# Hybrid decoder layer on one core: the norm's root of the first two chunks of x moved into TensorE's turning product

## The chip, the cores and the metric

The kernel runs on one core of one Trainium2 chip. The metric is the device time of one execution in microseconds, the median of several executions of the same program.

## What is computed

One decoder layer over 512 tokens of width 1024, in float32: a half-step SwiGLU feed-forward block, a token mixer with two kinds of recurrent heads, and a second half-step feed-forward block. Each block stands between two RMS norms. The change touches only the first norm and what follows at once from it.

```python
def rms_norm(x, g):
    y = x * lax.rsqrt(jnp.mean(x * x, axis=-1, keepdims=True) + EPS)
    return y * g

def swiglu_ffn(x, w_in, w_out):
    gate, up = jnp.split(x @ w_in, 2, axis=-1)
    return (jax.nn.silu(gate) * up) @ w_out

x = x + 0.5 * rms_norm(swiglu_ffn(rms_norm(x, norm_pre[0]), ffn1_w_in, ffn1_w_out), norm_post[0])
x = x +       rms_norm(token_mixer(rms_norm(x, norm_pre[1]), ...), norm_post[1])
x = x + 0.5 * rms_norm(swiglu_ffn(rms_norm(x, norm_pre[2]), ffn2_w_in, ffn2_w_out), norm_post[2])
```

## The kernel before

The 512 tokens lie in four chunks of 128, one token per partition, in the tile `xs` (chunk i is `xs[:, i, :]`, with 1024 values per token). Before a product the normed chunk must be turned, so that the 1024 features lie on the partitions. TensorE does this 128x128 block by block against the identity matrix (`turn`, line 353: `transpose`), four blocks, which are one half of a chunk, into one PSUM tile.

Every operand of a product is held as a float32r high part and a float32r low part: ScalarE casts the value (the high part), VectorE subtracts that from the value (the low part), and three products (high by high, high by low, low by high) replace one exact product. A piece of weights goes the same way (`split`: ScalarE's cast in line 283, VectorE's subtraction in line 285). One call of `prod` is 24 such matmuls of 256 columns (line 608).

The feed-forward input product is done in a Strassen-like way on 2x2 halves, so it begins with the products c1, c3, c2, c4 of the list `HEADS`, which need only the first two chunks (`xh[0]`, first half of the features, for c1 and c3; `xh[1]`, second half, for c2 and c4). `start` writes out by hand the order of everything up to there; its calls stand under `tc.manual_schedule()`, so each engine's queue is in the order of the code:

- `gain_pe` loads the norm's gain as one row and spreads it over the partitions with two products against a row of ones; VectorE copies them out (line 177).
- `norm(i)` calls `root` and `scaled`. `root` squares the two halves of a chunk on ScalarE with a sum along the row (line 442), GpSimd turns each sum into a mean (line 443) and takes the power -0.5 (line 447). `scaled` multiplies a half by that root and by the gain on VectorE (line 470).
- `part` is a generator with four steps for one half h of one chunk i: turn, ScalarE's cast (line 373), VectorE's subtraction (line 375), and a plain copy kept for later (line 377).
- `spin` multiplies the identity by itself into a spare PSUM tile; its result is not used (line 183).

The chunks 2 and 3 follow in the middle of the c products (`norm(2)`, `norm(3)`, `to_s`). Weight loads go through SyncE's DMA queue in the order of the code, and a load waits until its buffer's last reader is done.

Of the kernel before, what the change touches and what calls it, by code (L numbers as in the profile page):

```python
# [8 lines left out]
F32 = mybir.dt.float32  # L9
F32R = mybir.dt.float32r  # L10
AF = mybir.ActivationFunctionType
ALU = mybir.AluOpType
PSUM = bass.MemoryType.PSUM

P = 128
T = 512
D = 1024
# [4 lines left out]
EPS = 1e-6  # L22
# [96 lines left out]
class Layer:  # L119
# [43 lines left out]
    def gain_pe(self, tag, row):  # L163

        nc = self.nc
        g = self.cp.tile([P, D], F32, tag=tag, bufs=1, name=self.nm(tag))
        r = self.hf[0:1, 14:16, :].rearrange("p a t -> p (a t)")
        nc.sync.dma_start(r, row)
        one = self.st("one", P)[:1]
        nc.gpsimd.memset(one, 1.0)  # L170
        self.spare = self.ps()
        self.spin(2)
        for h in range(2):
            ps = self.ps()
            v = slice(512 * h, 512 * h + 512)
            nc.tensor.matmul(ps, one, r[:, v], start=True, stop=True)
            nc.vector.tensor_copy(g[:, v], ps)
        return g

    def spin(self, n):  # L180

# [3 lines left out]
    def mm3(self, ps, sh, sl, mh, ml, start, stop, **kw):  # L185
        mm = self.nc.tensor.matmul
        mm(ps, sh, mh, start=start, stop=False, **kw)  # L187
        mm(ps, sh, ml, start=False, stop=False, **kw)  # L188
        mm(ps, sl, mh, start=False, stop=stop, **kw)  # L189

    def xop(self, k, part, t0, t1):
        q = self.xq[2 * (t0 // HALF) + k // KH]
        return q[:, part, k % KH, t0 % HALF : (t1 - 1) % HALF + 1]
# [151 lines left out]
        nc.gpsimd.tensor_tensor(r, m, self.nhalf[:, :n], op=ALU.pow)  # L345
        return r

    def turn(self, src, h):

        pt = self.ps()  # L350
        for c in range(4):
            k = 4 * h + c
            self.nc.tensor.transpose(pt[:, c * P : (c + 1) * P], src[:, k * P : (k + 1) * P], self.ident)  # L353
        return pt.rearrange("p (c t) -> p c t", c=4)

    def two(self, dst, i, src):
# [7 lines left out]
        for h in halves:  # L364
            self.two(self.xq[2 * (i // 2) + h], i, self.turn(src, h))

    def part(self, i, h, src):

        pv = self.turn(src, h)
        v = slice(i * P, (i + 1) * P)  # L370
        dst = self.xh[h][:, :, :, v]
        yield
        self.nc.scalar.copy(dst[:, 0], pv)
        yield
        self.nc.vector.tensor_tensor(dst[:, 1], pv, dst[:, 0].bitcast(F32), op=ALU.subtract)
        yield
        self.nc.scalar.copy(self.xf[h][:, :, v], pv)
        yield
# [39 lines left out]
    def to_s(self, i, src):  # L418

        if i < 2:  # L420
            for h in range(2):
                g = self.part(i, h, src)
                for _ in range(3):
                    next(g)
                self.copies.append(g)
        else:
            self.gs.append(self.sums(i, src))
            next(self.gs[-1])
# [283 lines left out]
        self.hold = ()  # L712
        self.holes()

    def start(self, norm, xn):

        norm(0)
        norm(1)
        q = [[self.part(i, h, xn[i]) for h in range(2)] for i in range(2)]
        step = lambda *gs: [next(g) for g in gs]  # L720
        self.spin(3)
        step(q[0][0], q[0][1], q[0][0])
        self.spin(2)
        split = self.split()
        step(q[1][0], q[1][1])
        next(split)
        step(q[1][0])
        next(split)
        step(q[0][0], q[1][0])
        head = deque(HEADS)  # L730

        def prod():
            p, t = head.popleft()
            self.prod(p, t, False)
            return lambda: self.after(p, t)

        prod()
        self.full_split()
        step(q[0][1], q[1][1], q[0][1], q[1][1])
        prod()  # L740
        self.full_split()
        norm(2)
        c2 = prod()
        self.full_split()
        norm(3)
        step(q[0][0], q[0][1], q[1][0], q[1][1])
        self.full_split()
        self.to_s(2, xn[2])
        c4 = prod()
        c2()  # L750
        self.to_s(3, xn[3])
        p11 = prod()
        self.full_split()
        c4()
        self.lag()
        g2, g3 = self.gs
        prod()
        step(g2)
        p11()
        prod()  # L760
        step(g3)
        self.full_split()
        step(g2)
        e2 = prod()
        step(g3)
        p12 = prod()
        e2()
        self.full_split()
        step(g2)
        step(g3)  # L770
        p21 = prod()
        p12()
        e4 = prod()
        self.full_split()
        p22 = prod()
        p21()
        step(g2)
        step(g3)
        e4()
        self.lag()  # L780
        p22()
        self.holes()
# [1023 lines left out]
def layer(tc, aps):  # L1806
    with ExitStack() as ctx:
        L = Layer(ctx, tc, aps)
        nc = tc.nc
        x, out = aps["x"], aps["out"]  # L1810
        pre, post = aps["norm_pre"][0], aps["norm_post"][0]
        L.weights(
            L.ffn_items("f1", aps["ffn1_w_in"][0], aps["ffn1_w_out"][0]) + L.mix_items()
            + L.ffn_items("f2", aps["ffn2_w_in"][0], aps["ffn2_w_out"][0])
        )
        gp, xn, roots = [None], [None] * NT, {}

        def norm(i, row=None):
            if i == 0 and row is not None:
                gp[0] = L.gain("gpre", pre[row : row + 1, :])  # L1820
            xn[i] = L.pre(i, gp[0], row == 2 and i == NT - 1)

        def root(i):

            if i < 2:
                norm(i, 1)
            else:
                roots[i] = L.root(i)

        def scaled(i, h):  # L1830
            r, xn[i] = roots[i]
            L.scaled(i, gp[0], r, xn[i], h)

        def trans(i):
            L.to_t(i, xn[i])

        def trans_s(i):
            L.to_s(i, xn[i])

        def store(i):  # L1840
            for h in range(2):
                v = slice(512 * h, 512 * h + 512)
                nc.sync.dma_start(out[0, i * P : (i + 1) * P, v], L.xs[:, i, v])

        with ExitStack() as f1:
            L.open_ffn(f1)
            with tc.manual_schedule():
                first = L.start_loads()
                gp[0] = L.gain_pe("gpre", pre[0:1, :])
                for i in range(NT):  # L1850
                    for h in range(2):
                        v = slice(512 * h, 512 * h + 512)
                        (nc.scalar if i < 2 and h else nc.sync).dma_start(L.xs[:, i, v], x[0, i * P : (i + 1) * P, v])
                    if i:
                        L.load(first.popleft())
                    if i == 1:

                        nc.scalar.activation(L.col(), L.nhalf[:, :1], AF.Exp)
                while first:
                    L.load(first.popleft())  # L1860
                L.start(norm, xn)
            L.small_params()
            L.ffn_in()
            L.ffn_out(post[0:1, :], 0.5, root, trans, lambda trans: L.head4(trans, scaled))
        L.mixer()
        with ExitStack() as f2:
            L.open_ffn(f2, True)
            L.mix_out1(lambda i: norm(i, 2), trans_s, L.ffn_head)
            L.ffn_in()
            L.ffn_out(post[2:3, :], 0.5, store, lambda i: None, lambda trans: None)  # L1870
# [30 lines left out]
```

## Time and profile before

| | |
|---|---|
| time, median of 3 runs | 930.09 us (929.65 to 931.55) |
| the profiled execution's own time | 933.69 us |
| its span, first to last instruction | 932.0 us |
| TensorE busy | 921.7 us, 99% of the span |
| VectorE, ScalarE, GpSimd busy | 765.9, 525.2, 186.9 us |
| first product c1 begins | 14.05 us after the span's start |

The profiled execution is one execution with its own time, 3.6 us above the median of the others; sums over its rows are made against that time. In a row of the timeline stand the start, the duration, the engine, the line of the kernel, the operation, output and input, and in brackets how long the engine had been idle before it and what ended that. "PE" is TensorE's matmul, "PEld" its weight load, DVE is VectorE, ACT ScalarE, POOL GpSimd, SP SyncE (SPq is its DMA queue).

### The profile page before, as it was taken

Reading aid. Unit: us, or ns where it says so; the run is one execution under the profiler, and the core shown is the slowest. Engines: PE = TensorE matmul, PEld = TensorE weight load, DVE = VectorE, ACT = ScalarE, POOL = GpSimd, SP = SyncE. Lnnn points to the kernel's source line nnn. Section 1 sums busy time; section 2 is a strip of 40 time slices with the busy share of each in tenths; the row PEclk is TensorE's granted clock in tenths of the full one; section 3 lists DMA queues with packets and bytes.
Section 4 is the critical chain, followed back from the end, with each engine's and each line's share of the span. In section 5 each row is a group of like instructions: output and inputs, shape, how many; then the busy total and the mean of one; then the engine's idle time right before and its main releaser. Section 6 shows DMA issues by size and latency. Waiting matters only on the chain.

```text
span 932.0 us, 18308 instructions
## 1 busy us (share of the span) xinstructions
PE 921.7 (99%) x7423; PEld 887.4 (95%) x7423; DVE 765.9 (82%) x992; ACT 525.2 (56%) x757; POOL 186.9 (20%) x256
## 2 busy tenths in 40 slices
PE   8999999999999999999999999999999999999997
PEld 7999999999999999998887888899999999999997
DVE  5899978889888776698847564799898989998886
ACT  6645455557565466956633444495454545756661
POOL 3531112121111045452321210304000000011002
PEclk9999999999999999999999999999999999999999
DMA  9245679776797925798742124452453435279542
GB/s 310 76 138 157 181 182 214 195 157 142 209 273 238 262 65 150 151 184 208 152 98 69 46 72 132 137 162 66 135 159 123 136 111 174 84 221 261 165 153 91
DMA packets 118766, 145.42 MB, mean 156 GB/s; under 512 B 7413, under 2 KB 91417, under 8 KB 118682
## 3 DMA queue, kind: packets, MB, share of 16 engines
q1 hardware_dynamic: 102714, 129.05, 44.2%
q0 software_dynamic: 15680, 14.69, 11.6%
q8 instruction: 58, 0.95, 0.4%
q10 hardware_dynamic: 288, 0.52, 0.2%
q14 instruction: 26, 0.21, 0.1%
HBM read 142.14 MB, written 31.46 MB: 186 GB/s over the span
## 4 chain that ended last, share of the span: by engine, by line
PE 62%; ACT 1%; DVE 0%; issue 0%; POOL 0%; DVEq 0%; POOLq 0%; ACTq 0%
PE ps L608 22%; PE ps L955 8%; PE ps L538 6%; PE ps L187 5%; PE ps L189 5%; PE ps L188 5%; PE ps L947 4%; PE ps L1373 2%; PE ps L353 1%; PE ps L548 1%; PE ps L1466 0%; PE ps L1671 0%; PE ps L1644 0%; PE ps L1419 0%; PE ps L1668 0%; PE ps L1431 0%
## 5 line engine op out<-in xcount | busy, mean ns | idle before, releaser
L283 ACT CAST w<-raw 128x1024 fp32r<-128x1024 f32 x246 | 251.3, 1028 | 199.0 <-PE ps L608 93.6
L285 DVE TENSOR_TENSOR w<-raw,w 128x1024 fp32r<-128x1024 f32 x246 | 298.9, 1219 | 30.9 <-ACT w L283 29.5
L608 PE MATMUL ps<-xq,w 128*128 128x256 f32 x2016 | 237.1, 277 | 0.0
L608 PEld LDWEIGHTS ps<-xq,w 128*128 128x128 f32 x2016 | 232.9, 188 | 0.0
L608 PE MATMUL ps<-sq,w 128*128 128x256 f32 x1512 | 178.0, 276 | 0.3
L608 PEld LDWEIGHTS ps<-sq,w 128*128 128x128 f32 x1512 | 174.2, 188 | 1.0 <-ACT ps L659 0.9
L299 DVE TENSOR_TENSOR raw<-raw,raw 128x1024 f32<-128x1024 f32 x72 | 89.8, 1251 | 7.8 <-DMA raw<-in_ffn_w_in_dram 6.1
L955 PE MATMUL ps<-w,hs 128*128 128x256 f32 x672 | 81.0, 276 | 0.0
L947 PE MATMUL ps<-w,hs 128*128 128x256 f32 x672 | 79.2, 276 | 0.0
L955 PEld LDWEIGHTS ps<-w,hs 128*128 128x128 f32 x672 | 78.4, 188 | 0.0
L187 PE MATMUL ps<-w,xq 128*128 128x512 f32 x192 | 77.9, 407 | 0.1
L947 PEld LDWEIGHTS ps<-w,hs 128*128 128x128 f32 x672 | 77.5, 188 | 0.0
L189 PE MATMUL ps<-w,xq 128*128 128x512 f32 x192 | 74.8, 391 | 0.0
L188 PE MATMUL ps<-w,xq 128*128 128x512 f32 x192 | 74.8, 390 | 0.0
L538 PE MATMUL ps<-xq,w 128*128 128x256 f32 x480 | 57.5, 282 | 0.0
L538 PEld LDWEIGHTS ps<-xq,w 128*128 128x128 f32 x480 | 56.6, 189 | 0.5 <-issue 0.5
L887 POOL DMA_DIRECT2D f2sums<-in_ffn_w_out_dram x15 | 20.0, 1482 | 176.9 <-DMA f2sums<-in_ffn_w_out_dram 176.9
L827 ACT CAST hs<-hf 128x1024 fp32r<-128x1024 f32 x32 | 33.7, 1053 | 28.8 <-PE ps L955 21.1
L828 DVE TENSOR_TENSOR hs<-hf,hs 128x1024 fp32r<-128x1024 f32 x32 | 39.1, 1221 | 8.7 <-ACT hs L827 8.2
L887 POOL DMA_DIRECT2D f1sums<-f1sums x26 | 23.2, 892 | 105.9 <-DMA f1sums<-in_ffn_w_out_dram 53.0
L187 PEld LDWEIGHTS ps<-w,xq 128*128 128x128 f32 x192 | 36.1, 188 | 8.5 <-issue 1.0
L189 PEld LDWEIGHTS ps<-w,xq 128*128 128x128 f32 x192 | 36.1, 188 | 8.1 <-DVE xq L360 0.3
(262 smaller groups left out, 1223.3 us busy)
## 6 DMA issues: line engine op xcount, KB each, us to landing
raw<-in_ffn_w_in_dram SPq DMA_DIRECT2D x98, 512.0 KB, 5.3
raw<-in_ffn_w_out_dram SPq DMA_DIRECT2D x44, 512.0 KB, 4.5
raw<-in_w_mix_in_dram SPq DMA_DIRECT2D x28, 512.0 KB, 3.6
raw<-f2sums SPq DMA_DIRECT2D x15, 512.0 KB, 5.6
raw<-f1sums SPq DMA_DIRECT2D x13, 512.0 KB, 7.6
raw<-in_w_mix_out_dram SPq DMA_DIRECT2D x8, 512.0 KB, 3.7
f2sums<-in_ffn_w_out_dram SPq DMA_DIRECT2D x30, 128.0 KB, 5.9
f2sums<-in_ffn_w_out_dram SPq DMA_DIRECT2D x15, 256.0 KB, 5.7
```

What stands on the lines that cost most here:

```text
L187: mm(ps, sh, mh, start=start, stop=False, **kw)
L188: mm(ps, sh, ml, start=False, stop=False, **kw)
L189: mm(ps, sl, mh, start=False, stop=stop, **kw)
L283: nc.scalar.copy(hi, raw)
L285: self.low = nc.vector.tensor_tensor(lo, raw, hi.bitcast(F32), op=ALU.subtract)
L299: added = (nc.vector if late else nc.gpsimd).tensor_tensor(o, o, c, op=ALU.add)
L538: mm(ps[:, u0:u1], w[:, a, k, :], self.xop(k, b, u0, u1), start=k + n + m == 0, stop=k == ND - 1 and n == 2, skip_group_check=True,)
L608: self.nc.tensor.matmul(ps[:, c], wb[b][:, k, v], left[d][:, k, :], start=first and a + n + k == 0, stop=n == 2 and k == KH - 1, skip_grou ...
L828: self.nc.vector.tensor_tensor(lo, src, hi.bitcast(F32), op=ALU.subtract)
L887: nc.gpsimd.dma_start(to[:, a:b], v, accum_op=ALU.add)
L947: mm(out, a[kk][:, i * P : (i + 1) * P], w[:, b, kk, QUARTER * v : QUARTER * (v + 1)], start=begin and c == kk == n == 0, stop=kk == 1 and ...
L955: mm(ps[:, QUARTER * c : QUARTER * (c + 1)], A[a][:, c], B[b], start=begin and c == n == 0, stop=n == 2, skip_group_check=True,)
```

## The change

For chunks 0 and 1 only:

- ScalarE squares a chunk whole (`root_whole`: two instructions of 1024 columns instead of four of 512), and GpSimd makes one mean and one power of each.
- VectorE multiplies x by the gain alone (`scale`), half by half, without waiting for the root. The copy of the gain's second half comes after the first halves of both chunks (`rest`).
- VectorE multiplies the identity by the root, one root per partition (`diagonal`), and `turn` multiplies each block by this diagonal with an ordinary float32 `matmul` in place of `transpose`. The turned block comes out scaled.
- Only the first halves are turned before c1. The second halves of both chunks are turned between c1 and c3; VectorE's `scale(1, 1)` stands after the subtractions of the first halves.
- ScalarE's cast of the first piece of weights stands before the casts of the first halves, no longer between them.

```diff
     def gain_pe(self, tag, row):
...
-            nc.vector.tensor_copy(g[:, v], ps)
-        return g
+            copies.append(lambda v=v, ps=ps: nc.vector.tensor_copy(g[:, v], ps))
+        copies[0]()
+        return g, copies[1]
...
-    def turn(self, src, h):
+    def turn(self, src, h, diag=None):
...
-            self.nc.tensor.transpose(pt[:, c * P : (c + 1) * P], src[:, k * P : (k + 1) * P], self.ident)
+            out, block = pt[:, c * P : (c + 1) * P], src[:, k * P : (k + 1) * P]
+            if diag is None:
+                self.nc.tensor.transpose(out, block, self.ident)
+            else:
+                self.nc.tensor.matmul(out, block, diag, start=True, stop=True)
...
-    def start(self, norm, xn):
-
-        norm(0)
-        norm(1)
-        q = [[self.part(i, h, xn[i]) for h in range(2)] for i in range(2)]
+    def root_whole(self, i):
+
+        nc = self.nc
+        out = self.hf[:, 2 * i : 2 * i + 2, :].rearrange("p a t -> p (a t)")
+        ss, m, r = self.col(), self.col(), self.col()
+        nc.scalar.activation(out, self.xs[:, i, :], AF.Square, accum_out=ss)
+        nc.gpsimd.tensor_scalar(m, ss, 1.0 / D, EPS, op0=ALU.mult, op1=ALU.add)
+        nc.gpsimd.tensor_tensor(r, m, self.nhalf[:, :1], op=ALU.pow)
+        return r
+
+    def start(self, norm, xn, g, rest):
...
+        def scale(i, h):
+            v = slice(512 * h, 512 * h + 512)
+            nc.vector.tensor_tensor(src[i][:, v], self.xs[:, i, v], g[:, v], op=ALU.mult)
+
+        def diagonal(i):
+            nc.vector.tensor_scalar(diag[i], self.ident, roots[i], None, op0=ALU.mult)
+
+        scale(0, 0)
+        scale(1, 0)
+        rest()
+        roots = [self.root_whole(i) for i in range(2)]
+        diag = [self.st("diag", P) for _ in range(2)]
+        diagonal(0)
+        scale(0, 1)
+        diagonal(1)
+        q = [[self.part(i, h, src[i], diag[i]) for h in range(2)] for i in range(2)]
         step = lambda *gs: [next(g) for g in gs]
+        split = self.split()
+        next(split)
         self.spin(3)
-        step(q[0][0], q[0][1], q[0][0])
+        step(q[0][0], q[0][0])
         self.spin(2)
-        split = self.split()
-        step(q[1][0], q[1][1])
-        next(split)
-        step(q[1][0])
+        step(q[1][0], q[1][0])
         next(split)
         step(q[0][0], q[1][0])
+        scale(1, 1)
...
         prod()
         self.full_split()
-        step(q[0][1], q[1][1], q[0][1], q[1][1])
+        step(q[0][1], q[1][1], q[0][1], q[1][1], q[0][1], q[1][1])
```

On TensorE, from the last spins before the first turn to c2. Before (`xn_170` is the normed chunk 0, `hf_113` holds chunk 1, `ps_220` is c1 and then c2, `ps_253` is c3):

```order
4 L183 MATMUL ps_131<-ident 128x128 x3
5 L353 MATMUL ps_190<-ident,xn_170 128x128 x4
6 L353 MATMUL ps_195<-ident,xn_170 128x128 x4
7 L183 MATMUL ps_131<-ident 128x128 x2
8 L353 MATMUL ps_203<-ident,hf_113 128x128 x4
9 L353 MATMUL ps_208<-ident,hf_113 128x128 x4
10 L608 MATMUL ps_220<-xq_78,sq_116 128x256 x24
11 L608 MATMUL ps_253<-xq_78,sq_114 128x256 x24
12 L608 MATMUL ps_220<-xq_75,w 128x256 x24
```

The same place after the change (`xn_157` and `hf_113` hold the two chunks times the gain, `diag_173` and `diag_174` the diagonals, `ps_202` is c1 and then c2, `ps_245` is c3):

```order
4 L185 MATMUL ps_131<-ident 128x128 x3
5 L359 MATMUL ps_182<-diag_173,xn_157 128x128 x4
6 L185 MATMUL ps_131<-ident 128x128 x2
7 L359 MATMUL ps_190<-diag_174,hf_113 128x128 x4
8 L614 MATMUL ps_202<-xq_78,sq_116 128x256 x24
9 L359 MATMUL ps_231<-diag_173,xn_157 128x128 x4
10 L359 MATMUL ps_236<-diag_174,hf_113 128x128 x4
11 L614 MATMUL ps_245<-xq_78,sq_114 128x256 x24
12 L614 MATMUL ps_202<-xq_75,w 128x256 x24
```

The turns of the two second halves moved from ahead of c1 to between c1 and c3, and all four turns are now products with a diagonal.

On VectorE, from the first copy of the gain to the subtraction for the second piece of weights. Before (`sq_116` and `sq_114` are the pieces of weights of c1 and c3, `xq_78` is the turned first half):

```order
1 L177 COPY gpre_127<-ps_134 128x512
2 L177 COPY gpre_127<-ps_137 128x512
3 L470 SCALAR_TENSOR_TENSOR xn_170<-xs,col_168,gpre_127 128x512 x2
4 L470 SCALAR_TENSOR_TENSOR hf_113<-xs,col_183,gpre_127 128x512 x2
5 L285 TENSOR_TENSOR sq_116<-raw_119,sq_116 128x1024
6 L375 TENSOR_TENSOR xq_78<-ps_190,xq_78 128x4x128
7 L375 TENSOR_TENSOR xq_78<-ps_203,xq_78 128x4x128
8 L285 TENSOR_TENSOR sq_114<-raw_121,sq_114 128x1024
```

After the change:

```order
1 L178 COPY gpre_127<-ps_134 128x512
2 L739 TENSOR_TENSOR xn_157<-xs,gpre_127 128x512
3 L739 TENSOR_TENSOR hf_113<-xs,gpre_127 128x512
4 L178 COPY gpre_127<-ps_136 128x512
5 L742 TENSOR_SCALAR diag_173<-ident,col_163 128x128
6 L739 TENSOR_TENSOR xn_157<-xs,gpre_127 128x512
7 L742 TENSOR_SCALAR diag_174<-ident,col_169 128x128
8 L287 TENSOR_TENSOR sq_116<-raw_119,sq_116 128x1024
9 L381 TENSOR_TENSOR xq_78<-ps_182,xq_78 128x4x128
10 L381 TENSOR_TENSOR xq_78<-ps_190,xq_78 128x4x128
11 L739 TENSOR_TENSOR hf_113<-xs,gpre_127 128x512
12 L287 TENSOR_TENSOR sq_114<-raw_121,sq_114 128x1024
```

The four multiplications by root and gain became four by the gain alone, two of them ahead of the root; two small products of the identity with a root came in, and the last half of chunk 1 moved behind the subtractions of the first halves.

On SyncE's queue three loads changed places: the two small loads `gb` and the gain of the norm behind the block (`gpost`, 512 KB) now stand before two pieces of weights (`raw_37`, `raw_316`) that they followed.

More of the change, by code (lines that the diff above doesn't have):

```diff
@@ L172, in gain_pe @@
         self.spin(2)
+        copies = []
         for h in range(2):
@@ L365, in to_t, with part @@
             self.two(self.xq[2 * (i // 2) + h], i, self.turn(src, h))
-    def part(self, i, h, src):
-        pv = self.turn(src, h)
+    def part(self, i, h, src, diag):
+        pv = self.turn(src, h, diag)
         v = slice(i * P, (i + 1) * P)
@@ L421, in to_s @@
             for h in range(2):
-                g = self.part(i, h, src)
+                g = self.part(i, h, src, None)
                 for _ in range(3):
@@ L713, in ffn_head @@
         self.holes()
-    def start(self, norm, xn):
-        norm(0)
-        norm(1)
-        q = [[self.part(i, h, xn[i]) for h in range(2)] for i in range(2)]
+    def root_whole(self, i):
[7 more added lines that the diff above has]
+    def start(self, norm, xn, g, rest):
+        nc = self.nc
+        src = [self.sp.tile([P, D], F32, tag="xn", bufs=1, name=self.nm("xn"))]
+        src.append(self.hf[:, 16:18, :].rearrange("p a t -> p (a t)"))
+        def scale(i, h):
[12 more added lines that the diff above has]
+        q = [[self.part(i, h, src[i], diag[i]) for h in range(2)] for i in range(2)]
         step = lambda *gs: [next(g) for g in gs]
+        split = self.split()
+        next(split)
         self.spin(3)
-        step(q[0][0], q[0][1], q[0][0])
+        step(q[0][0], q[0][0])
         self.spin(2)
-        split = self.split()
-        step(q[1][0], q[1][1])
-        next(split)
-        step(q[1][0])
+        step(q[1][0], q[1][0])
         next(split)
         step(q[0][0], q[1][0])
+        scale(1, 1)
         head = deque(HEADS)
@@ L1848, in layer @@
                 first = L.start_loads()
-                gp[0] = L.gain_pe("gpre", pre[0:1, :])
+                gp[0], rest = L.gain_pe("gpre", pre[0:1, :])
                 for i in range(NT):
@@ L1860, in layer @@
                     L.load(first.popleft())
-                L.start(norm, xn)
+                L.start(norm, xn, gp[0], rest)
             L.small_params()
```

## The prediction, written before the changed kernel ran

> **What bounds the kernel now.** I read the page's sums first, then the windows, then what TensorE waits for.
>
> ```profile
> span 932.0 us, 18308 instructions
> PE 921.7 (99%) x7423; PEld 887.4 (95%) x7423; DVE 765.9 (82%) x992; ACT 525.2 (56%) x757; POOL 186.9 (20%) x256
> ...
> 0.00:14.05 14.05, 10.54 (x35) 7.24 (x35) 5.64 (x8) 6.55 (x14) 3.99 (x17) 1.00 0.84 284
> 14.05:400.00 385.95, 385.75 (x3369) 384.70 (x3370) 326.47 (x392) 236.56 (x328) 104.55 (x129) 1.00 0.67 178
> ...
> 500.00:925.00 425.00, 424.56 (x3347) 406.73 (x3345) 353.06 (x469) 230.95 (x346) 44.46 (x72) 1.00 0.43 133
> ...
> PE ps L353 <- DVE xn L470: 1.7, 1, 1.7
> PE ps L183 <- POOL ident masks.py:199: 1.6, 1, 1.6
> PE ps L608 <- ACT xq L373: 0.2, 1, 0.2
> ```
>
> From 14.05 us on, where the first product c1 begins, TensorE (first busy column) works 385.75 of 385.95 us, later 424.56 of 425. All its named waits lie before 14.05. So the time is the start of c1, plus TensorE's work behind it, plus a tail that the change does not touch. A microsecond less before c1 is a microsecond won, and a microsecond of TensorE work put behind c1 is one lost, unless something waits there.
>
> The timeline of the opening shows how c1's start comes about.
>
> ```profile
> 6.39 0.63 ACT L442 ACTIVATE junk<-xs 128x512 f32<-128x512 f32 x1 [3.20 <-DMA xs<-in_x_dram]
> 6.42 1.65 PE L183 MATMUL ps<-ident 128*128 128x128 f32 x6
> 6.53 0.69 DVE L177 COPY gpre<-ps 128x512 f32<-128x512 f32 x1 [1.02 <-PE ps L176]
> 7.14 0.63 ACT L442 ACTIVATE junk<-xs 128x512 f32<-128x512 f32 x1
> 7.68 0.19 ACT L442 ACTIVATION_READ_ACCUMULATOR junk<-xs 128x1 f32 x1
> 8.39 0.56 POOL L447 TENSOR_TENSOR col<-col,nhalf 128x1 f32<-128x1 f32 x1
> 8.98 1.41 DVE L470 SCALAR_TENSOR_TENSOR xn<-xs,col,gpre 128x512 f32<-128x512 f32 x2 [1.76 <-POOL col L447]
> 9.03 0.75 POOL L443 TENSOR_SCALAR col<-col 128x1 f32<-128x1 f32 x1
> 9.79 1.97 PE L353 MATMUL ps<-ident,xn 128*128 128x128 f32 x8 [1.72 <-DVE xn L470]
> 11.42 1.05 ACT L283 CAST sq<-raw 128x1024 fp32r<-128x1024 f32 x1
> 11.55 1.06 PE L183 MATMUL ps<-ident 128*128 128x128 f32 x4
> 12.40 1.41 PE L353 MATMUL ps<-ident,hf 128*128 128x128 f32 x8
> 13.41 0.59 ACT L373 CAST xq<-ps 128x512 fp32r<-128x512 f32 x1 [0.94 <-PE ps L353]
> 14.05 5.83 PE L608 MATMUL ps<-xq,sq 128*128 128x256 f32 x48 [0.24 <-ACT xq L373]
> ```
>
> x arrives at 6.39; squares, mean and power give VectorE the root at 8.98; TensorE turns from 9.79. From there TensorE itself is the chain: 8 transposes and 4 spin instructions take 9.79 to 12.40 (the four spins 12.40 - 11.55 = 0.85, 0.213 us each); chunk 1's first half follows, ScalarE casts it at 13.41, and c1 starts 0.64 us later. c1 and c3 (x48) run without a gap between them.
>
> **The change part by part.** First, what a turn costs now.
>
> ```profile
> L183 PE MATMUL ps<-ident 128*128 128x128 f32 x14 | 3.9, 443 | 1.6 <-POOL ident masks.py:199 1.6
> L176 PE MATMUL ps<-hf,one 1*128 1x512 f32 x4 | 3.8, 1096 | 0.0
> 441.14 1.95 PE L1419 MATMUL ps<-q,kk 128*128 128x128 f32 x16
> 442.85 0.48 PE L187 MATMUL ps<-w,xq 128*128 128x512 f32 x1
> 22.44 1.03 PE L353 MATMUL ps<-ident,xn 128*128 128x128 f32 x8
> ```
>
> The code spins 7 times, and the group has 14 instructions; the gain is spread by 2 products, with 4. An ordinary float32 product is thus two passes, where eight transposes are eight instructions. Later in the kernel a pass is faster: 16 passes of 128x128 take 442.85 - 441.14 = 1.71 us, 0.107 each, half of the 0.213 in the opening. The eight transposes at 22.44 (1.03 us) against those at 9.79 (1.97) say the same. Each turned half therefore grows from 4 passes to 8.
>
> *Start of c1.* Squaring whole: a half takes 0.63; a cast of 1024 columns takes 1.05 where one of 512 takes 0.59, so the whole square takes about 0.63 + 0.46 = 1.09 and its sum is read out by 6.39 + 1.09 + 0.10 = 7.58, against 7.87 for the second half before. From 7.87 to VectorE's 8.98 it took 1.11 us; the same gives 8.69. VectorE has by then done two `scale` halves and the gain's second copy (three times 0.69 from 6.39: 8.46). The diagonal is a quarter of such a copy's columns; no row shows one, so it lies between 0 and 0.69, and I take 0.25 by the column count. TensorE starts at 9.0, 0.8 us earlier. But before, c1 needed 4 + 4 + 4 + 4 = 16 slow passes (two turned halves, spins, one half); now it needs 8 + 4 + 8 = 20. Before: 9.79 + 16 x 0.213 = 13.20, cast at 13.41. Now: 9.0 + 20 x 0.213 = 13.26, cast at 13.47, c1 at 14.11. **Term: +0.06.** The 0.8 us gained ahead of the turns go into four more passes.
>
> Chunk 1's root does not decide: its mean may wait beside VectorE's `scale(0, 1)`, as the 0.75 us of POOL's 9.03 row beside the 8.98 row shows, so its diagonal comes at about 10.5; TensorE gets to it only at 9.0 + 12 x 0.213 = 11.6.
>
> When TensorE speeds up matters too. The eight transposes at 12.40 took 1.41, between 1.97 and 1.03: the pace changed at about 13.1, 3.3 us after TensorE's steady work began at 9.79 (the granted clock reads 1.00 throughout and does not show it). If the change comes 3.3 us after steady work begins, it comes at 12.3 now, and the 0.96 us of passes behind it halve: c1 0.5 earlier, and the sum below is +1.5. If it comes at the same moment as before, the sum stands at +2.0. I take the second, as spins ran in both just ahead, and keep the first as the lower end. [...]
>
> *The second halves.* Before, TensorE turned chunk 0's second half in passes already counted, and chunk 1's while it would have waited for the cast. Now both stand between c1 and c3, where it never waited: 2 x 4 blocks x 2 passes = 16 passes of 128x128, the same as the 441.14 row. **Term: +1.71.** Slow passes would make it 3.4, but by 17 us the pace is the fast one.
>
> *What is late behind.* ScalarE and VectorE do the rest of the opening in a fixed order, and these rows are its slack.
>
> ```profile
> 14.84 1.07 ACT L373 CAST xq<-ps 128x512 fp32r<-128x512 f32 x2
> 15.80 1.07 ACT L283 CAST w<-raw 128x1024 fp32r<-128x1024 f32 x1
> 19.62 1.42 DVE L470 SCALAR_TENSOR_TENSOR xn<-xs,col,gpre 128x512 f32<-128x512 f32 x2 [1.09 <-POOL col L447]
> 20.95 1.22 DVE L285 TENSOR_TENSOR sq<-raw,sq 128x1024 fp32r<-128x1024 f32 x1
> 22.19 0.37 SPq L244 DMA_DIRECT2D raw<-in_ffn_w_in_dram  x1
> 22.88 1.41 DVE L470 SCALAR_TENSOR_TENSOR hf<-xs,col,gpre 128x512 f32<-128x512 f32 x2 [0.72 <-POOL col L447]
> 26.14 1.04 PE L353 MATMUL ps<-ident,hf 128*128 128x128 f32 x8
> 31.56 4.89 POOL L299 TENSOR_TENSOR raw<-raw,raw 128x1024 f32<-128x1024 f32 x2 [1.16 <-DVE w L285]
> ```
>
> The casts of the second halves (14.84) now wait for their turns: c1 ends at about 16.8, the turns at 18.6, the second cast at 19.3, where the next piece's cast started at 15.80 before. What queues behind them on ScalarE, the squares of chunks 2 and 3 above all, is 3.5 us later. Chunk 2, scaled by 21.04 before, is scaled by about 24.5; TensorE wants to turn it at 22.44 + 1.77 = 24.2. A slack of 1.4 us becomes a wait of 0.3, give or take as much: **term +0.2** (0 to 0.6). Chunk 3, scaled by 24.3, comes at 27.8 against a turn at 26.14 + 2.0 = 28.1: just in time.
>
> *The rest costs nothing.* ScalarE's cast of the first weights now stands ahead of the first halves' casts and waits for a transfer:
>
> ```profile
> 2.08 0.43 SPq L244 DMA_DIRECT2D raw<-in_ffn_w_in_dram  x1
> DMA to landing us min/median/max: 6.8/7.7/8.8
> ```
>
> It lands between 8.9 and 11.3, is cast by 12.4 at the latest, and the cast that c1 needs comes at 13.47. VectorE's `scale(1, 1)` (0.7) has until c1 ends. SyncE's load that was issued at 22.19, when VectorE's row of 20.95 had freed its buffer, goes out at about 25.7 behind the gain's 512 KB and lands by 34.9; POOL's second addition in the 31.56 row is its first reader, at 34.0 before and about 37 now.
>
> *Sum.* 0.06 + 1.71 + 0.2 = +2.0 us. The profiled execution would go from 933.69 (span 932.0 and 1.7 around it) to 935.7. It lies 3.6 above the median of the runs shown; I carry the difference over: 930.09 + 2.0 = **932.1**. A measurement of this kernel can tell about 0.2%, 1.86 us, from no change, so this stands just beyond it.
>
> **The rivals.**
>
> *The fast pace comes a whole stretch earlier (not slower), 0.20.* TensorE now pauses only from 8.07 to 9.0 between spins and turns, not to 9.79, and everything it does is a full product. If that suffices to bring the pace up by 9.75, 16.5 of the 20 passes take 0.107: 9.75 + 1.77 = 11.5, c1 at 11.5 + 0.85 = 12.4, and -1.65 + 1.71 + 0.2 = +0.3: 930.4. It decides if the pace changes before about 11. Against it: 8 transposes and 4 spin instructions were enough to bring it up before. [...]
>
> *x arrives earlier in the other executions (slower still), 0.17.* They are 3.6 us faster than the profiled one, whose ScalarE waited for x until 6.39. With x there by 4.4, TensorE turns once the spins end at 8.07, in both kernels; then c1 starts at 8.07 + 3.41 + 0.85 = 12.3 before and 8.07 + 4.26 + 0.85 = 13.2 now. +0.85 + 1.71 + 0.2 = +2.8: 932.9.
>
> *More waits behind, 0.08.* ScalarE is 3.5 us late and TensorE 2.0; wherever less than 1.5 us of slack is left, TensorE waits. Chunk 3 has 0.3. Up to 1 us more: 933.1.
>
> *The product with the diagonal is one pass, like a transpose, 0.05.* Then c1 needs 12 passes: 9.0 + 2.56 + 0.85 = 12.4, and the second halves cost 0.86: -1.65 + 0.86 + 0.2 = -0.6, 929.5. The 14 instructions of 7 spins speak against it.
>
> **How the numbers follow.** The forecast has 0.50, with its own range +1.3 to +2.6 (the earlier pace, the wait of 0 to 0.6). Range for 8 in 10: from the early pace with a little less, 930.0, to the largest of the slower cases, 933.3. Slower by over 0.2%: about 0.62 of the forecast's 0.50, and the 0.17 and 0.08, 0.56. Faster by over 0.2% takes an early pace and a cheap turn together, or something not seen here: 0.07. Within: 0.37.
>
> **What would show it.** Right: TensorE's turns start near 9.0 with x8 in place of x4 instructions a half, c1 within 0.3 of 14.1, a row of 16 product instructions taking 1.7 between c1 and c3, chunk 2's turn waiting for VectorE. Wrong: c1 before 13, the fast pace ahead of 11, the second halves' turns under 1 us, or idle time on TensorE in front of c3.

## The result and the profile after

| | |
|---|---|
| kernel before, median of 6 runs | 930.57 us (929.65 to 931.55) |
| changed kernel, median of 6 runs | 935.72 us (933.0 to 937.5) |
| ratio | 1.0053, interval 1.0035 to 1.0072 |
| profiled execution of the changed kernel | 935.71 us, span 934.0 us |

The change costs 5.15 us where 2.0 were predicted, and the median lies 2.4 us above the range. First the page's sums for the changed kernel (busy time of each engine).

```profile
span 934.0 us, 18329 instructions
PE 924.0 (99%) x7439; PEld 889.3 (95%) x7439; DVE 767.4 (82%) x994; ACT 524.5 (56%) x753; POOL 185.5 (20%) x254
```

Its windows with c1's start as the cut (length, then busy time of PE, PEld, DVE, ACT, POOL, granted clock, DMA share, GB/s):

```profile
13.52:400.00 386.48, 386.30 (x3370) 384.92 (x3371) 326.64 (x391) 234.52 (x326) 103.94 (x130) 1.00 0.68 178
```

What TensorE waits for (total, times, longest), but for the identity at the start:

```profile
PE ps L359 <- DVE diag L742: 0.8, 1, 0.8
PE ps L614 <- ACT xq L379: 0.7, 1, 0.7
```

TensorE is still full from c1 on (386.30 of 386.48), so the bound was read rightly. It pauses twice ahead of c1: 0.8 us for the diagonal, 0.7 for the cast. The timeline of the opening says why.

```profile
4.83 1.06 ACT L726 ACTIVATE hf<-xs 128x1024 f32<-128x1024 f32 x1 [1.64 <-DMA xs<-in_x_dram]
6.48 0.56 POOL L728 TENSOR_TENSOR col<-col,nhalf 128x1 f32<-128x1 f32 x1
7.36 0.69 DVE L739 TENSOR_TENSOR hf<-xs,gpre 128x512 f32<-128x512 f32 x1 [1.12 <-DMA xs<-in_x_dram]
7.97 0.68 DVE L178 COPY gpre<-ps 128x512 f32<-128x512 f32 x1
8.57 0.28 DVE L742 TENSOR_SCALAR diag<-ident,col 128x128 f32<-128x128 f32 x1
8.91 2.07 PE L359 MATMUL ps<-diag,xn 128*128 128x128 f32 x8 [0.83 <-DVE diag L742]
13.52 3.02 PE L614 MATMUL ps<-xq,sq 128*128 128x256 f32 x24 [0.68 <-ACT xq L379]
16.38 1.05 PE L359 MATMUL ps<-diag,xn 128*128 128x128 f32 x8
18.08 3.05 PE L614 MATMUL ps<-xq,sq 128*128 128x256 f32 x24
```

Here x of chunk 0 is squared from 4.83, not from 6.39 as in the execution that the prediction was worked from, and the root of chunk 0 is out by 7.04. But VectorE stands at chunk 1's product (7.36) and waits 1.12 us for chunk 1's x; the gain's copy and the diagonal come behind it in its queue. So TensorE turns from 8.91, when it could have turned at 8.0, the end of its spins (before_again, below). The second halves of both chunks cost 18.08 - 16.38 = 1.70.

### The profile page after: what moved, and what is told of

Its sections match the earlier page's. It is cut to its first block, busy times and chain, and to the rows that moved or that the text cites. A ratio compares the mean times of both kernels' runs of the same rounds, so it can differ in the third digit from the quotient of the medians.

```text
span 934.0 us, 18329 instructions
## 1 busy us (share of the span) xinstructions
PE 924.0 (99%) x7439; PEld 889.3 (95%) x7439; DVE 767.4 (82%) x994; ACT 524.5 (56%) x753; POOL 185.5 (20%) x254
## 4 chain that ended last, share of the span: by engine, by line
PE 56%; DVE 3%; issue 1%; POOL 1%; ACT 1%; DMA 1%; DVEq 0%; POOLq 0%; ACTq 0%
PE ps L614 16%; PE ps L988 8%; PE ps L544 6%; PE ps L189 5%; PE ps L191 5%; PE ps L190 5%; PE ps L980 4%; PE ps L1406 2%; DVE w L287 1%; PE ps L554 1%; POOL raw L301 1%; PE ps L357 1%; DVE raw L301 1%; DMA raw<-in_ffn_w_in_dram 1%; PE ps L1499 0%
```

## The experiments

These explanations stand against each other in the expectations. A: the profiled execution of the kernel before had a late x and others don't, and the changed kernel is held by chunk 1's x on VectorE. B: executions differ only in the moment at which TensorE's passes become fast; P, in later expectations: pauses on TensorE move that moment. C: waits behind c1. The kernel before was measured again beside every set; its medians there were 930.81, 931.27, 931.27 and 932.03 us.

**Both kernels again.** *before_again* is the kernel before, *after_again*, *after_timed* and *after_x1_late* are the changed kernel, all four unaltered (the last label means a base for the kernels with a later x below).

> The kernel before, unchanged, for a second profile of it and as a measure of how far two sets of executions of one program lie apart (ratio 1.000, within 0.1%). Theory A (x comes earlier in most executions than in the profile shown, and the kernel before uses that while the changed one does not): this profile has the first square before 5.5 us and c1 before 12.8, and its own time is nearer 930.5 than 933.7. Theory B (only the moment of the fast pace differs between executions): the first square again near 6.4, c1 near 14, the own time moved by the pace alone. Theory C (waits behind c1 make the difference): c1 as in the first profile, own time near 933.7.

> The changed kernel, unchanged, for a second profile. In the first one TensorE's first turn began at 8.91, after VectorE had waited until 7.36 for chunk 1's first half, and the pace rose at about 12. Theory A: the first turn again waits for chunk 1's half, whatever chunk 0 does, so it begins 8.5 to 9.2; c1 13 to 14.2; own time 933 to 937.5. Theory B: the own time goes with the pace alone, about 0.5 us for each us that the pace rises later. Theory C: named waits of TensorE behind c1.

> The changed kernel once more, unaltered, timed in rounds beside the kernel before: how wide its executions scatter, and its own x4.x profile for a third time. [...]

> The changed kernel unaltered (the name notwithstanding), as the base for the next one on the same chip. Theory A: its time follows the landing of chunk 1's first half: 933.4 to 934.5 with the first turn at 7.9 to 8.1 if that lands by 6.3, 935 to 936.5 with the first turn at 8.7 or later if it lands by 7.2.

before_again took 931.04 us (ratio 1.0002, 0.9993 to 1.001); its profiled execution has a span of 929.3 against the first one's 932.0. Its timeline:

```profile
4.62 0.63 ACT L442 ACTIVATE junk<-xs 128x512 f32<-128x512 f32 x1 [1.43 <-DMA xs<-in_x_dram]
8.02 1.97 PE L353 MATMUL ps<-ident,xn 128*128 128x128 f32 x8
10.63 1.70 PE L353 MATMUL ps<-ident,hf 128*128 128x128 f32 x8
12.36 5.84 PE L608 MATMUL ps<-xq,sq 128*128 128x256 f32 x48
```

x is there at 4.62, TensorE turns at once when its spins end at 8.02, and c1 starts at 12.36, not 14.05. The execution behind the prediction was one with a late x. The changed kernel took 936.1 (one execution), 933.87 (ratio 1.003, 1.0018 to 1.0041) and 933.41 (1.0023, 1.0011 to 1.0034). Chunk 1's product, the first turn and c1 in the timelines, of after_again, of after_timed and of after_x1_late:

```profile
7.24 0.69 DVE L739 TENSOR_TENSOR hf<-xs,gpre 128x512 f32<-128x512 f32 x1 [1.00 <-DMA xs<-in_x_dram]
8.78 2.08 PE L359 MATMUL ps<-diag,xn 128*128 128x128 f32 x8 [0.71 <-DVE diag L742]
13.75 3.11 PE L614 MATMUL ps<-xq,sq 128*128 128x256 f32 x24 [0.68 <-ACT xq L379]
```

```profile
6.19 0.69 DVE L739 TENSOR_TENSOR hf<-xs,gpre 128x512 f32<-128x512 f32 x1
7.89 1.92 PE L359 MATMUL ps<-diag,xn 128*128 128x128 f32 x8
11.88 3.05 PE L614 MATMUL ps<-xq,sq 128*128 128x256 f32 x24 [0.68 <-ACT xq L379]
```

```profile
6.24 0.68 DVE L739 TENSOR_TENSOR hf<-xs,gpre 128x512 f32<-128x512 f32 x1
7.95 1.91 PE L359 MATMUL ps<-diag,xn 128*128 128x128 f32 x8
12.44 3.10 PE L614 MATMUL ps<-xq,sq 128*128 128x256 f32 x24 [0.68 <-ACT xq L379]
```

One kernel, two kinds of opening: with chunk 1's x at 7.24 the first turn waits 0.71 for the diagonal and c1 is 1.39 behind before_again's; with x at 6.19 or 6.24 it waits for nothing, and c1 is 0.48 ahead or 0.08 behind. That chunk 1's x can hold the first turn is shown by that; the 0.56 between the two early ones is mostly the pace: TensorE's passes became fast at about 9.8 in after_timed (four spins in 0.71 us from 9.60) and at about 10.9 in after_x1_late (four in 1.06 from 9.66, then the eight passes of chunk 1 in 1.26 from 10.51; at the fast pace eight take 1.06).

Two expectations missed. after_timed was to have a median of 935.0 to 936.5, and had 933.87 with executions 1.8 us apart. And after_x1_late's profiled execution, with its early first turn, was to take 933.4 to 934.5, and took 935.47, 2.1 over the median of its own set. So the landing of chunk 1's x alone doesn't tell how long an execution takes.

**One line moved on VectorE.** *x1_behind* is the changed kernel with chunk 1's product behind chunk 0's diagonal:

```diff
         scale(0, 0)
-        scale(1, 0)
         rest()
...
         diagonal(0)
+        scale(1, 0)
```

> The changed kernel with the product of chunk 1's first half and the gain moved behind chunk 0's diagonal on VectorE, so that chunk 1's x no longer stands in front of chunk 0's turn. Theory A (that order costs the time before c1 and, through the pause on TensorE, the early pace): 1 to 2 us faster than the changed kernel, ratio to before 1.003 to 1.004; first turn by 8.1 when the spins end. Theory B or C: as the changed kernel, ratio 1.005.

It took 932.98 us (1.0028, 1.0017 to 1.0039), beside 936.1 of after_again on the same chip. But 936.1 is one execution, and the unaltered kernel stands as near to the kernel before in the other two sets (1.003 and 1.0023). So no gain in time is shown here. TensorE didn't wait for a diagonal (timeline), but chunk 1's first half may have been early, too:

```profile
7.97 1.81 PE L359 MATMUL ps<-diag,xn 128*128 128x128 f32 x8
```

**Chunk 1's x made later.** In *before_x1_late* (kernel before), *after_x1_later* (changed) and *x1_behind_later* (x1_behind) its first half is issued behind the first weight load, not ahead of it:

```diff
                 for i in range(NT):
+                    if i == 1:
+                        L.load(first.popleft())
                     for h in range(2):
...
-                    if i:
+                    if i > 1:
                         L.load(first.popleft())
```

> The kernel before with one thing moved: chunk 1's first half of x is issued behind the first weight load instead of ahead of it, so that it lands about 1.3 us later (7.4 to 8.5 where the traces so far show 5.8 to 7.3). Chunk 1's turn came 3.9 us after its squares began in the trace of before_again (6.74 to 10.63), 0.85 of it filled by spins. Theory A (chunk 1's x decides only where it stands ahead of chunk 0's diagonal): c1 0 to 0.9 later than 12.36, median 0 to 1.2 over the kernel before.

> The changed kernel with chunk 1's first half of x issued behind the first weight load, about 1.3 us later. Theory A: VectorE stands at the product of chunk 1's first half until it lands and does the gain's copy (0.69) and the diagonal (0.28) only then, so that the first turn starts 1.5 us after the landing, at 9.0 to 10.0, with a pause of 1 to 2 us on TensorE ahead of it, and c1 6.5 us after the landing, at 14 to 15; median 3.5 to 6.5 over the kernel before, 2 to 3.5 more than the same shift costs the kernel before. Theory C (fixed waits behind c1): no more than the kernel before loses by the shift.

> x1_behind (the product of chunk 1's first half behind chunk 0's diagonal on VectorE) with the same later landing. Theory A: the first turn stays at 8.0, the filling products lie ahead of the landing's effect, c1 0.3 to 0.9 later than its 11.80, median 1.8 to 3.2 over the kernel before and at least 1.5 under after_x1_later. Theory C: the same as after_x1_later.

They took 932.87 (1.0016, 1.0006 to 1.0026), 935.83 (1.0045, 1.0028 to 1.0061) and 933.51 us (1.003, 1.0019 to 1.0041). The shift costs the kernel before 1.6 (0 to 1.2 were expected), the changed one 2.4 (from 933.41). That is 0.8 more, where I had expected 2 to 3.5 more: a miss. With the product behind the diagonal the time is 2.3 lower on the same chip (933.51 against 935.83; at least 1.5 was expected). The timelines, of after_x1_later and then of x1_behind_later:

```profile
9.34 0.69 DVE L739 TENSOR_TENSOR hf<-xs,gpre 128x512 f32<-128x512 f32 x1 [2.99 <-DMA xs<-in_x_dram]
10.55 0.27 DVE L742 TENSOR_SCALAR diag<-ident,col 128x128 f32<-128x128 f32 x1
10.88 2.07 PE L359 MATMUL ps<-diag,xn 128*128 128x128 f32 x8 [2.70 <-DVE diag L742]
16.18 3.10 PE L614 MATMUL ps<-xq,sq 128*128 128x256 f32 x24 [0.68 <-ACT xq L379]
```

```profile
7.86 1.77 PE L359 MATMUL ps<-diag,xn 128*128 128x128 f32 x8
7.96 0.69 DVE L739 TENSOR_TENSOR hf<-xs,gpre 128x512 f32<-128x512 f32 x1 [0.55 <-DMA xs<-in_x_dram]
12.30 3.04 PE L614 MATMUL ps<-xq,sq 128*128 128x256 f32 x24 [0.68 <-ACT xq L379]
```

The diagonal comes 1.21 us behind the product's start in both executions with a late x (7.36 to 8.57, 9.34 to 10.55), and TensorE waits for it; in x1_behind_later it turns at 7.86, before chunk 1's x is there at 7.96. So the hold on VectorE is shown, and that the order is worth time when x is late. My 1.5 us from landing to first turn held (9.34 to 10.88). The x came later than I thought here, and the same edit left it at 7.96 in the other execution, so the two c1 compare the order and the landing together.

**The second halves alone.** *late_halves* and *late_again* are the kernel before (transposes, split squares) with only the second halves turned late; *late_filled* is the same with three pauses of TensorE filled by unused products (the notes behind # say where; they don't stand in the code).

```diff
         self.spin(3)            # late_filled: spin(5)
-        step(q[0][0], q[0][1], q[0][0])
+        step(q[0][0], q[0][0])
         self.spin(2)            # late_filled: spin(3)
...
-        step(q[1][0], q[1][1])
+        step(q[1][0])
...
         step(q[0][0], q[1][0])  # late_filled: spin(3) behind it
...
-        step(q[0][1], q[1][1], q[0][1], q[1][1])
+        step(q[0][1], q[1][1], q[0][1], q[1][1], q[0][1], q[1][1])
```

> The kernel before with one part of the change alone: the second halves of chunks 0 and 1 are turned (by transposes of the normed chunk, as before) between c1 and c3. It moves 8 one-pass blocks behind c1, 0.86 us by the fast pace, and takes 4 passes from in front of c1 (0.4 to 0.85) if the roots are there in time. Theory A or B: +0.3 to +0.9 us, ratio 1.000 to 1.001. Theory C (the casts that wait behind the late turns make TensorE wait): +1.5 to +2.5 us, ratio 1.002 to 1.003.

> late_halves once more, as the base for late_filled on the same chip. Theory P: in the executions in which TensorE's pauses (0.4, 0.3 and 0.7 us ahead of c1) move the change of pace behind c1, c1's 24 passes take 5.5 us instead of 2.9: 933 to 936 with a scatter of 5 us or more. Theory C: 933 to 936 with a scatter like the kernel before's (4 us or less).

> late_halves with the three pauses filled by passes that nothing uses (two filling products more ahead of the first turn, one more ahead of chunk 1's, three ahead of c1; 12 instructions). Theory P: the fast pace comes by 13 us in every execution, c1's 24 passes take 2.9 to 3.1 us, c1 at 12.3 to 13.3, median 931.8 to 933.3 and the slowest executions under 935, though TensorE runs 12 passes more. Theory C: no gain, 0 to 1 us slower than late_again.

late_halves took 934.36 us (1.004, 1.0023 to 1.0057; 931.2 to 939.12), late_again 934.18 (1.0025, 1.0011 to 1.0039; 931.46 to 937.2), late_filled 932.34 (1.0006, 0.9996 to 1.0016; 931.16 to 934.39). I had expected 0.3 to 0.9 over the kernel before for the first and missed. Twelve instructions more on the full engine made it 1.8 us faster. What TensorE waits for in late_halves:

```profile
PE ps L608 <- ACT xq L373: 0.7, 1, 0.7
PE ps L353 <- DVE xn L470: 0.4, 1, 0.4
PE ps L353 <- DVE hf L470: 0.3, 1, 0.3
```

The timelines, of late_halves, of late_again and of late_filled:

```profile
12.48 5.49 PE L608 MATMUL ps<-xq,sq 128*128 128x256 f32 x24 [0.67 <-ACT xq L373]
17.77 0.72 PE L353 MATMUL ps<-ident,xn 128*128 128x128 f32 x4
```

```profile
12.14 3.05 PE L608 MATMUL ps<-xq,sq 128*128 128x256 f32 x24 [0.68 <-ACT xq L373]
```

```profile
11.71 3.19 PE L608 MATMUL ps<-xq,sq 128*128 128x256 f32 x24 [0.19 <-ACT xq L373]
```

In late_halves, with three pauses, c1's 24 passes took 5.49 us: the pace rose only at about 18, in the turns behind c1. In late_again, the same kernel with the same three pauses, they took 3.05 (932.85 us, below its median), so the pauses don't always do it. With the pauses filled the pace was up by c1 (3.19 us for its 24), which started at 11.71, earlier than the 12.3 to 13.3 I had named, and the executions lie 3.2 us apart, where they lay 5.7 and 7.9 apart. This agrees with P: pauses move the rise in a part of the executions. That each of the longest executions is of this kind was seen in one trace only.

*fill_pauses* did the same to the changed kernel (`spin(5)` ahead of the first turn, `spin(3)` ahead of c1).

> The changed kernel with the two pauses of TensorE filled by passes that nothing uses: five instead of three of the filling products ahead of the first turn, and three more ahead of c1. Theory P (pauses move the change of pace): the fast pace comes by about 10 us in every execution, c1 at 13.0 to 13.8, median 933.0 to 934.5 and a scatter of 2.5 us or less, though TensorE has 10 passes more to run. Theory C, or the late x alone: nothing gained, 935.7 to 936.8.

It took 933.63 us (1.0025, 1.0014 to 1.0036), after_timed on the same chip 933.87: not to be told apart. Its c1 came at 12.93 (13.0 to 13.8 expected). Only the pause of 0.7 ahead of c1 was there to be filled, as x was early. It doesn't decide on P.

**The root in the product alone.** *x1_behind_early* is x1_behind with the second halves ahead of c1 again, as in the kernel before; VectorE's `scale(1, 1)` moves up behind `diagonal(1)` for it.

```diff
         diagonal(1)
+        scale(1, 1)
...
-        step(q[0][0], q[0][0])
+        step(q[0][0], q[0][1], q[0][0])
...
-        step(q[1][0], q[1][0])
+        step(q[1][0], q[1][1], q[1][0])
...
-        step(q[0][1], q[1][1], q[0][1], q[1][1], q[0][1], q[1][1])
+        step(q[0][1], q[1][1], q[0][1], q[1][1])
```

> x1_behind (the product of chunk 1's first half moved behind chunk 0's diagonal on VectorE) and in addition the second halves turned ahead of c1, as in the kernel before; what is left of the change is the root in the turning product and the whole squares. The 16 further passes of the float32 products stay. If they alone make the rest of the loss: c1 at 14.0 to 14.6, no passes between c1 and c3, the wait near 46 us gone as well (0.25), median 932.3 to 933.3, that is 1.5 to 2.5 over the kernel before. If the late second halves cost by themselves (waits behind c1, theory C): 930.8 to 931.8.

It took 931.99 us (1.0011, 1.0002 to 1.002), 0.7 over the kernel before: less than the 1.5 to 2.5 I had named for the further passes, and above the 930.8 to 931.8 named for theory C. Its timeline has c1 at 13.03, not at 14.0 to 14.6, and only 0.67 behind before_again's.

```profile
7.87 3.15 PE L359 MATMUL ps<-diag,xn 128*128 128x128 f32 x16
11.29 1.95 PE L359 MATMUL ps<-diag,hf 128*128 128x128 f32 x16
13.03 5.84 PE L614 MATMUL ps<-xq,sq 128*128 128x256 f32 x48
```

The 16 products of chunk 1 ran at the fast pace (1.95), so the further passes were cheap, and the second halves fill the time in which the late ones leave TensorE waiting 0.7 us for the cast.

**The whole squares alone.** *whole_squares* and *whole_again* are the kernel before with a root from one square of 1024 columns, and without the two spins between the turns.

```diff
-        *_, r = self.rms(parts[::-1] if turned else parts)
...
+        if self.whole:   # set in start for chunks 0 and 1 alone
...
+            ss, m, r = self.col(), self.col(), self.col()
+            self.square = nc.scalar.activation(out, x, AF.Square, accum_out=ss)
+            nc.gpsimd.tensor_scalar(m, ss, 1.0 / D, EPS, op0=ALU.mult, op1=ALU.add)
+            self.pow = nc.gpsimd.tensor_tensor(r, m, self.nhalf[:, :1], op=ALU.pow)
+        else:
+            *_, r = self.rms(parts[::-1] if turned else parts)
...
-        self.spin(2)
```

> The kernel before with only the squares in whole chunks (root of chunks 0 and 1 from one activation of 128x1024 each), and without the two filling products between the two turns; transposes, order and halves as before. Chunk 1's root then comes about 0.3 us earlier, and TensorE turns chunk 1 at once behind chunk 0. If x is there early and the pace keeps: c1 at 11.4 to 11.9 instead of 12.36, median 930.0 to 930.6 (0.3 to 0.9 under the kernel before). Theory P: TensorE pauses 0.2 to 0.5 us for chunk 1's scaled rows, and in a part of the executions the pace changes later: median 930.8 to 932.5 with a wider scatter.

> whole_squares once more, to see whether it beats the kernel before. By its first trace c1 starts at 11.51 instead of 12.36: 0.85 us less, 930.2 to 930.6 against some 931.1, ratio 0.999 to 0.9995; if that gain is lost again behind c1, or in executions with a late x: 1.000.

They took 931.05 (0.9997, 0.9988 to 1.0006) and 930.53 us (0.9989, 0.9978 to 1.0). The timeline of whole_again:

```profile
7.93 1.97 PE L353 MATMUL ps<-ident,xn 128*128 128x128 f32 x8
9.80 1.41 PE L353 MATMUL ps<-ident,hf 128*128 128x128 f32 x8
11.46 5.82 PE L616 MATMUL ps<-xq,sq 128*128 128x256 f32 x48 [0.24 <-ACT xq L373]
```

c1 starts 0.90 us earlier than in before_again. It is the best version found; the two sets put its gain at 0.2 and 1.5 us, and the first interval includes no gain at all, so it is at the edge of what twelve runs can tell (0.3 to 0.9 was expected). Whether squares or spins bring it was not separated.

## Why the prediction was wrong

- **The bound: right.** In the profiled execution of the result TensorE stands still for 0.2 of the 386 us from c1 to 400. Short waits behind c1 exist in some traces (0.9 us for VectorE at 676 in before_x1_late, 0.2 for ScalarE in late_again).
- **Start of c1 (+0.06): the step that failed.** It was worked from an execution whose chunk 0 came at 6.39, and the sum was then carried to a median whose executions have it at about 4.6. That case was among the rivals, with 0.17 and +2.8; it should have been the forecast, since 3.6 us between the profiled execution and the median had to be explained first. Its c1 before (12.3) was right to 0.06. The late x is 1.7 of the 3.6. Another part is a slow stretch of that execution: the same 288 products, from about 355 us on, take 34.09 us in it and 32.80 in before_again (timelines, first the earlier profile).

```profile
355.60 34.09 PE L538 MATMUL ps<-xq,w 128*128 128x256 f32 x288
```

```profile
353.81 32.80 PE L538 MATMUL ps<-xq,w 128*128 128x256 f32 x288
```

- **Chunk 1's x ahead of the diagonal: overlooked.** I had VectorE free by 8.46, working the three instructions from 6.39 without a wait, and did not ask when chunk 1's x lands. The rival's c1 of 13.2 came out at 13.52 and 13.75 with a late chunk 1, and at 11.88 and 12.44 with an early one.
- **Second halves (+1.71): right,** 1.70 in the trace.
- **Chunk 2's turn waits for VectorE (+0.2): right.** The wait stands with TensorE's weight load for that turn (timeline of the changed kernel):

```profile
23.85 0.86 PEld L357 LDWEIGHTS ps<-ident,xn 128*128 128x128 f32 x8 [0.20 <-DVE xn L476]
```

- **More waits behind: a rival with 0.08, right in kind.** The waits of TensorE's weight loads between 30 and 60 us in the changed kernel show one that before_again has not.

```profile
PEld ps L614 <- ACT hf L641: 0.3, 1, 0.3
```

- **Pace.** "The same moment as before" and "3.3 us after steady work" are both too simple: see below. The rival's rise by 9.75 was an estimate of mine; in the four traces of the changed kernel it came between about 9.8 (after_timed) and 12.4 (after_again, whose eight passes from 11.51 on took 1.57 us).
- **A stretch of slower passes: not thought of.** In windows of the same 10 us, after_again first, TensorE gets fewer passes done though it never stops:

```profile
60.00:70.00 10.00, 10.00 (x87) 1.00 0.71 217
```

```profile
60.00:70.00 10.00, 10.00 (x91) 1.00 0.89 266
```

All traces of kernels that turn the second halves late with products can be laid beside before_again by two points: c1, and a row of 48 products that begins at 340.54 us there.

```profile
340.54 6.12 PE L548 MATMUL ps<-xq,w 128*128 128x256 f32 x48
```

| trace | c1 later by | the 48 products later by | lost between | passes from 60 to 70 us |
|---|---|---|---|---|
| after (the result) | 1.16 | 3.43 | 2.27 | 91 |
| after_again | 1.39 | 4.83 | 3.44 | 87 |
| after_timed | -0.48 | 2.95 | 3.43 | 87 |
| after_x1_late | 0.08 | 3.53 | 3.45 | 87 |
| after_x1_later | 3.82 | 6.17 | 2.35 | 90 |
| x1_behind | -0.56 | 1.72 | 2.28 | 91 |
| x1_behind_later | -0.06 | 3.30 | 3.36 | 87 |
| fill_pauses | 0.57 | 3.96 | 3.39 | 88 |

Two things can be read from it. Behind c1 the change costs 2.3 us in every trace, where the forecast had 1.9: the further 0.4 is for the most part the wait of 0.3 shown above. And five of the eight traces lose another 1.1 us, just those with 87 or 88 passes from 60 to 70 us; the nine traces of the other kernels have 90 or 91 there. Whether the change brings this stretch on is not shown, and its cause is open.

So the cost is 2.3 us behind c1, plus what c1 itself moves (in the changed kernel -0.5 and +0.1 where chunk 1 was early, 1.2 and 1.4 where it was late), plus 1.1 in some executions. In after_again these are 4.8 of the 5.1 by which its span is longer than before_again's; behind 340 us the traces scatter by a microsecond or more. The 5.15 us are not a constant of the change: two other sets of the same kernel came out at 2.1 and 2.6 us (933.41 and 933.87 against 931.27), near the predicted difference, from a base that was 1.2 us higher. Of the six executions behind the 5.15 only one was profiled. It had chunk 1 late and the slow stretch behind 355 us (34.09 us for the 288 products there, too); how many of the other five had either is open, and so is why this set is 2 us slower than the later ones.

The turns did start near 9.0 with 8 instructions a half, as named ahead, but for another reason; c1 was not within 0.3 of 14.1. It was luck, too, that the profiled execution took 935.71, where the prediction had 935.7 for it: c1 came 0.53 earlier than in the first profile, not 0.06 later, and the waits behind and the scatter made up for it.

## What to carry to other kernels

When the profiled execution is well off the median, first find what was unusual in it (here a late transfer, and a stretch of slower passes), and work the sum for the usual execution. In an in-order queue, look at every instruction that is put ahead of one on the critical path and ask what it waits for, not only how long it runs: here a product of 0.69 us was free until its x came 1 us late. Pauses before TensorE has reached its pace may cost more than their length (in one trace 1.4 us of pauses went with 2.4 us more for c1), and unused products in them can pay for themselves (late_filled took 932.34 us, late_again 934.18).

## What the runs showed of the hardware

- **The moment of the fast pace is not fixed to the kernel's work.** In before_again it fell in chunk 1's transposes, at about 12 (10.63, 8 in 1.70 us); before_x1_late, with the same instructions up to there, ran its four spins fast at 9.55. The timeline of that kernel:

```profile
7.93 1.78 PE L353 MATMUL ps<-ident,xn 128*128 128x128 f32 x8
9.55 0.61 PE L183 MATMUL ps<-ident 128*128 128x128 f32 x4
```

  In the openings without a pause ahead of the rise it lies between about 9.2 (x1_behind_later, eight passes in 1.77 us from 7.86) and 12 (before_again); with pauses it came as late as 13.1 (the first profile, eight transposes in 1.41 us from 12.40) and 18 (late_halves, four in 0.72 us from 17.77). These moments are estimates from rows that are part slow, part fast: eight transposes took 1.97 us slow and 1.03 fast. A rise came among transposes alone, too: in whole_again TensorE does nothing else from 7.93 until c1, the first eight take 1.97 us and the second eight 1.41, so the pace rises at about 10.5. What sets the moment is not shown.
- **A transfer landed 1 to 2 us later** in one execution than in another of the same program: chunk 0's squares start at 6.39 and 4.62, chunk 1's product in the changed kernel at 7.36 and 6.19.
- **Stretches in which passes took some 4% longer,** at a granted clock of 1.00, came in a part of the executions. They were seen at two places: from about 50 to 80 us, about 1.1 us in all, in five traces of the changed kernel and its variants (87 or 88 passes from 60 to 70 us, against 90 or 91); and from about 355 us on, in the first profiles of both kernels (288 products in 34.09 us, against 32.80 in before_again). Their cause is open.
